# Row statistics, gain tiles and one step's order at the start of a hybrid decoder block

## The chip, the cores and the metric

The kernel runs on one core of one Trainium2 chip. The metric is the device time of one execution in microseconds (us). A core has five engines with their own instruction streams, each worked through in order: TensorE (PE; PEld is its weight load), VectorE (DVE), ScalarE (ACT), GpSimd (POOL) and SyncE (SP), which here only issues DMAs. SP, ACT and POOL issue DMAs, each into a queue of its own.

## The reference, cut to what matters

16 meta rows are put ahead of the 1024 rows of x (1040 rows of 1024 numbers). Each row is normalized and multiplied by a gain, and the result goes through one input projection and all that follows (a pooling mixer, forgetting attention with 8 heads, gates, an output projection, a residual and a final norm).

```python
def rmsnorm(x, g):
    xf = x.astype(jnp.float32)
    xf = xf * lax.rsqrt(jnp.mean(xf * xf, axis=-1, keepdims=True) + RMS_EPS)
    return (xf * g.astype(jnp.float32)).astype(x.dtype)

def hybrid_layer(x, norm_g, w_in, ...):
    h = rmsnorm(x, norm_g)
    proj = jnp.einsum('bld,dn->bln', h, w_in)
    u_pool, z_pool, q, k, v, z_attn, f_logit, g_pool, g_attn = jnp.split(proj, _split_points(), axis=-1)
    y_pool = causal_multiscale_pool(u_pool, pool_w, pool_scale) * jax.nn.silu(z_pool)
    ...
    y_attn = forgetting_attention(q, k, v, log_f).reshape(B, L, ATTN_WIDTH) * jax.nn.silu(z_attn)
    merged = (jax.nn.sigmoid(g_pool) * jnp.einsum('blc,cd->bld', y_pool, w_up_pool)
              + jax.nn.sigmoid(g_attn) * jnp.einsum('blc,cd->bld', y_attn, w_up_attn))
    return x + jnp.einsum('bld,de->ble', merged, w_out)
```

The kernel multiplies in pieces: every float32 operand is split into a high part and a low part, and a product is the sum of high by high, high by low and low by high.

## The kernel before, in words

The 1040 rows are cut into nine row tiles: tile 0 holds the 16 meta rows and 112 rows of x, tiles 1 to 7 hold 128 rows each, and tile 8 holds the last 16 rows. A row tile `xt` goes through these steps:

- `norm_load(i)` issues its load from SP's queue. Tile 0 has two loads: x (L184) and the meta rows (L185).
- `norm_stat` squares the row on ScalarE and sums it (L192, an activation and a read-out of the sum), adds epsilon on VectorE (L125) and takes the power -1/2 on GpSimd (L126). The tile `junk` takes the squares, which nobody reads.
- `norm_scale` multiplies, on VectorE, each half of the row by the statistic and by the gain (L197). The gain stands in PSUM as `gb`, spread over all 128 partitions by a matmul of ones with the row of gains (L399).
- `norm_t` transposes the tile on TensorE in two halves of four 128x128 blocks (L218; for the 16 rows of tile 8 L205, eight small ones), copies each half from PSUM as its high part `hh` on ScalarE (L220, L209) and takes the low part `hl` on VectorE (L221, L210). The halves use the two PSUM buffers `pt` of the pool psT in turn, and every third one the buffer `pn` of the pool psG: of tile 6 both halves go to `pt`, of tile 7 the first to `pn` and the second to `pt`. A buffer is free again when hh and hl of its former contents have been taken.

At the start ScalarE issues the load of the gains (L388) and does a tiny Square (L389), which brings its table load. The loads of row tiles 0 and 1 follow. TensorE does four dummy matmuls, the two for the gains, and one more (L395, L399). SP goes on with the raw weights of query, key and value of the first head pair (L404) between tiles 2 and 3. The weights are split into `whi` on ScalarE (L409) and `wlo` on GpSimd (L414).

Then a loop over twelve steps n = 0 to 11 projects query, key and value in turn for four stretches of rows (matmuls at L163, three groups of eight for each step: hh by whi, hl by whi, hh by wlo). The results are taken out of PSUM at L249 and L253 (query: `qa` on ScalarE, `ql` on VectorE), L271 and L274 (key: `ka` on both), and L278 (value: `vt` on ScalarE). After steps 4, 7 and 10, two blocks of the value are transposed (L287) and split into `V` (L292 on ScalarE, L293 on VectorE). In between, the loop handles the later row tiles:

```python
        i = {0: 2, 1: 3, 3: 4, 4: 5, 6: 6, 7: 7}.get(n)
        if i is not None:
            norm_t(i, xts[i], ntok(i))
        ...
        i = {1: 4, 2: 5, 4: 6, 5: 7, 6: 8}.get(n)
        if i is not None:
            norm_scale(xts[i], ntok(i), norm_stat(xts[i], ntok(i)))
```

So tile 7 is scaled at the end of step 5, tile 6 transposed in step 6, tile 8 scaled at the end of step 6, tile 7 transposed in step 7. The transposes of tile 8 stand inside step 8, after its first eight matmuls. Step 9 is the first that reads the rows of tiles 6 to 8.

All of this stands in a `manual_schedule` of all engines: each engine executes these instructions in the order of the program text. Behind it, only TensorE's order is written by hand (a planner inserts projection work between the steps of attention, by fixed costs); the other engines' instructions there are ordered by the framework's scheduler.

Of the kernel before, what the change touches and what calls it, by code (L numbers as in the profile page):

```python
# [8 lines left out]
F32 = mybir.dt.float32  # L9
F32R = mybir.dt.float32r  # L10
AF = mybir.ActivationFunctionType
ALU = mybir.AluOpType
AX = mybir.AxisListType

D = 1024
NM = 16
# [4 lines left out]
EPS = 1e-6  # L21
# [24 lines left out]
def r32(ap):  # L46
    return ap.bitcast(F32)
# [7 lines left out]
def tile_hybrid_block(ctx, tc, x, meta, norm_g, w_in, b_forget, pool_w, pool_scale,  # L55
                      w_up_pool, w_up_attn, w_out, final_g, out):
    nc = tc.nc
# [20 lines left out]
    sm = ctx.enter_context(tc.tile_pool(name="sm", bufs=2))  # L78
# [8 lines left out]
    psG = G_.enter_context(tc.tile_pool(name="psG", bufs=1, space=PS))  # L87
# [4 lines left out]
    epsp = cst.tile([128, 1], F32, name="epsp")  # L92
# [29 lines left out]
    def rstd_of(ss):  # L122
        n = ss.shape[0]
        r = sm.tile([128, 1], F32, name="rstd", bufs=4)
        nc.vector.tensor_scalar(r[:n], ss, EPS, None, op0=ALU.add)  # L125
        nc.gpsimd.tensor_tensor(r[:n], r[:n], epsp[:n], op=ALU.pow)  # L126
        return r
# [44 lines left out]
    def run(g):  # L172
        for _ in g:
            pass

    gb = psG.tile([128, 2, 512], F32, name="gb")
    junk = gp.tile([128, D], F32, name="junk", tag="g")

    def norm_load(i):
        c0 = i * 128  # L180
        n = min(128, L - c0)
        xt = ap_.tile([128, D], F32, name="xt", tag="s", bufs=6)
        if i == 0:
            nc.sync.dma_start(xt[NM:], x2[:128 - NM, :])  # L184
            nc.sync.dma_start(xt[:NM], meta)  # L185
        else:
            nc.sync.dma_start(xt[:n], x2[c0 - NM:c0 - NM + n, :])
        return xt

    def norm_stat(xt, n):  # L190
        ss = sm.tile([128, 1], F32, name="ss")
        nc.scalar.activation(junk[:n], xt[:n], AF.Square, scale=D ** -0.5, accum_out=ss[:n])  # L192
        return rstd_of(ss[:n])

    def norm_scale(xt, n, r):
        for j, (c0, c1) in enumerate(HALVES):
            nc.vector.scalar_tensor_tensor(xt[:n, c0:c1], xt[:n, c0:c1], r[:n], gb[:n, j],  # L197
                                           op0=ALU.mult, op1=ALU.mult)

    def norm_t(i0, xt, n):  # L200
        c0 = i0 * 128
        if n < 128:
            both = psT.tile([128, KO, n], F32, name="pt")
            for i in range(KO):
                nc.tensor.transpose(both[:, i, :], xt[:n, i * 128:(i + 1) * 128], ident[:n, :n])  # L205
            for j in range(2):
                h_ = hh4[j][:, :, c0:c0 + n]
                part = both[:, 4 * j:4 * j + 4]
                nc.scalar.activation(h_, part, AF.Copy)  # L209
                last = nc.vector.tensor_tensor(hl4[j][:, :, c0:c0 + n], part, r32(h_), op=ALU.subtract)  # L210
            return last
        for j in range(2):
            if (2 * i0 + j) % 3 == 2:
                pt = psG.tile([128, 4, 128], F32, name="pn")
            else:
                pt = psT.tile([128, 4, 128], F32, name="pt")
            for i in range(4):
                nc.tensor.transpose(pt[:, i, :n], xt[:n, (4 * j + i) * 128:(4 * j + i + 1) * 128], ident[:n, :n])  # L218
            h_ = hh4[j][:, :, c0:c0 + n]
            nc.scalar.activation(h_, pt[:, :, :n], AF.Copy)  # L220
            last = nc.vector.tensor_tensor(hl4[j][:, :, c0:c0 + n], pt[:, :, :n], r32(h_), op=ALU.subtract)  # L221
        return last
# [6 lines left out]
    def zero_q(p):  # L229
        for e in range(2):  # L230
            nc.gpsimd.memset(r32(QL[p, e])[rows(e)[1]], 0.0)
# [12 lines left out]
    def q_piece(p, w, t0, t1):  # L244
        c0, c1 = t0 - NM, t1 - NM
        ps = yield from g_proj(w, t0, t1)

        def hi(e, r):
            nc.scalar.activation(QA[p, e][r, c0:c1], ps[rows(e)[0]], AF.Copy, scale=0.125)  # L249

        def lo(e):
            a, _ = rows(e)
            nc.vector.scalar_tensor_tensor(QL[p, e][a, c0:c1], ps[a], 0.125, r32(QA[p, e][a, c0:c1]),  # L253
                                           op0=ALU.mult, op1=ALU.subtract)

        for group in EVAC[p > 0]:
            for e in group:
                hi(e, rows(e)[0])
                if not p:
                    hi(e, rows(e)[1])  # L260
            for e in group:
                lo(e)
                if p:
                    hi(e, rows(e)[1])

    def k_piece(p, w, t0, t1):
        ps = yield from g_proj(w, t0, t1)
        for group in EVAC[p > 0]:
            for e in group:
                a, o = rows(e)  # L270
                nc.scalar.activation(KA[p, e][a, t0:t1], ps[a], AF.Copy)  # L271
            for e in group:
                a, o = rows(e)
                nc.vector.tensor_tensor(KA[p, e][o, t0:t1], ps[a], r32(KA[p, e][a, t0:t1]), op=ALU.subtract)  # L274

    def v_piece(p, w, t0, t1):
        ps = yield from g_proj(w, t0, t1)
        nc.scalar.activation(VT[p][:, t0:t1], ps, AF.Copy)  # L278

    def v_alloc(p):  # L280
        for e in range(2):
            V[p, e] = ap_.tile([KB, NB, 2, 64], F32R, name="V", bufs=3)
# [102 lines left out]
    onesr = ap_.tile([128, 128], F32R, name="onesr", tag="m")  # L385
    nc.vector.memset(r32(onesr), 1.0)
    grow = ap_.tile([1, D], F32, name="grow", tag="t")
    nc.scalar.dma_start(grow, norm_g)  # L388
    nc.scalar.activation(junk[:1, :2], r32(onesr)[:1, :2], AF.Square)  # L389
    xts = {0: norm_load(0), 1: norm_load(1)}  # L390
    warm = psG.tile([128, 4, 128], F32, name="pn")

    def warm_up(n):
        for _ in range(n):
            nc.tensor.matmul(warm, onesr, onesr[:, None, :].to_broadcast([128, 4, 128]), start=True, stop=True)  # L395

    warm_up(WARM[0])
    for j, (c0, c1) in enumerate(HALVES):
        nc.tensor.matmul(gb[:, j], r32(onesr)[:1], grow[:, c0:c1], start=True, stop=True)  # L399
    warm_up(WARM[1])  # L400

    def load_raw(col, pool=None, tag="raw"):
# [4 lines left out]
    def split_hi(raw, pool, tag):  # L407
        hi = pool.tile([128, KO, 128], F32R, name="whi", tag=tag)
        nc.scalar.activation(hi, raw, AF.Copy)  # L409
        return hi  # L410

    def split_lo(raw, hi, pool, tag):
        lo = pool.tile([128, KO, 128], F32R, name="wlo", tag=tag)
        nc.gpsimd.tensor_tensor(lo, raw, r32(hi), op=ALU.subtract)  # L414
        return hi, lo

    rq = load_raw(COL_Q)
    xts[2] = norm_load(2)
    rk = load_raw(COL_K)
    xts[3] = norm_load(3)  # L420
    rv = load_raw(COL_V, gp, "g")

    def ntok(i):
        return min(128, L - 128 * i)

    alloc_k(0)
    for i in range(2):
        norm_scale(xts[i], 128, norm_stat(xts[i], 128))
    hq_ = split_hi(rq, wp, "wh")
    norm_t(0, xts[0], 128)  # L430
    wq = split_lo(rq, hq_, wp, "wl")
# [4 lines left out]
    for i in (2, 3):  # L436
        norm_scale(xts[i], 128, rs[i - 2])
# [4 lines left out]
    for n, (kind, t0, t1) in enumerate(todo):  # L442
        if n + 4 < 9:
            xts[n + 4] = norm_load(n + 4)
        if kind == "q":
            run(q_piece(0, wq, max(NM, t0), t1))
        elif kind == "k":
            run(k_piece(0, wk, t0, t1))
        else:
            g = v_piece(0, wv, t0, t1)  # L450
            if n == 8:
                for _ in range(KO):
                    next(g)
                norm_t(8, xts[8], ntok(8))
            run(g)
# [3 lines that stand above are left out]
        if n == 0:  # L459
            hv_ = split_hi(rv, gp, "g")  # L460
            wv = split_lo(rv, hv_, gp, "g")
            VT[0] = gp.tile([128, L], F32, name="vt", tag="g")
            v_alloc(0)
        i = {1: 4, 2: 5, 4: 6, 5: 7, 6: 8}.get(n)
        if i is not None:
            norm_scale(xts[i], ntok(i), norm_stat(xts[i], ntok(i)))
        if n == 2:
            zero_q(0)
        if n == 4:
            wf = at_.tile([128, KO, H], F32, name="wf", bufs=1)  # L470
            nc.sync.dma_start(wf, w_in2[:, :, COL_F:COL_F + H])
        if n == 8:
            wfs = at_.tile([128, KO, 2 * H], F32R, name="wfs", bufs=1)
            nc.vector.tensor_copy(wfs[:, :, :H], wf)
            nc.vector.tensor_tensor(wfs[:, :, H:], wf, r32(wfs[:, :, :H]), op=ALU.subtract)
        if n in (4, 7, 10):
            run(v_blocks(0, 2 * (n // 3) - 2, 2 * (n // 3)))
# [507 lines left out]
    for n, s in enumerate(steps):  # L985
# [10 lines left out]
        j, a = s  # L996
# [148 lines left out]
```

## Time and profile before

| what | value |
|---|---|
| time, 3 runs | 737.64, 738.9 and 739.29 us, median 738.9 |
| the profiled execution: time | 738.82 us |
| the profiled execution: span, first to last instruction | 737.1 us |
| granted TensorE clock, mean | 0.999 |
| TensorE busy | 725.2 us, 98% of the span |
| VectorE, ScalarE, GpSimd busy | 531.6, 375.8, 305.9 us |
| input stage (to the last projection of the first head pair) | 0 to 56.5 us |

A row of the timeline has the start in us, the duration of the group in us, the engine (a "q" behind it is its queue, where DMAs are issued), the line, the operation, the tile written and the tiles read, shapes, and the number of instructions. A bracket at its end is the idle time of the engine ahead of it, and what ended that. A row of the busy time by stage has the stretch, its length, and for TensorE, its weight load, VectorE, ScalarE and GpSimd the busy time with the count, then the granted clock, the share of time in which the DMA engines were busy, and GB/s. A row of the DMA issues has the KB of each and the time from issue to landing in us. A row of the groups has the line, the shapes, the count, the busy time in us and the mean in ns of one instruction, then the idle time ahead.

### The profile page before, as it was taken

What the parts mean: (1) busy time and instruction counts of PE and PEld (TensorE: products, weight loads), DVE (VectorE), ACT (ScalarE), POOL (GpSimd) and SP (SyncE); (2) the same over time, 40 slices, a digit from 0 to 9 for tenths busy, and PEclk for the clock granted to TensorE, in tenths of its full rate; (3) what the DMA queues carried; (4) which work ended last, traced back from release to release, by engine and by line L of the source; (5) the groups of instructions that cost most, each with busy time, mean ns of one, the idle gap of its engine ahead of it and who ended that gap; (6) DMA issues with size and microseconds to landing.
All of it is one profiled execution on the core that took longest, in us unless ns stands there. A gap on an engine that the chain in (4) does not pass through costs nothing.

```text
span 737.1 us, 10620 instructions
## 1 busy us (share of the span) xinstructions
PE 725.2 (98%) x3686; PEld 624.2 (85%) x3686; DVE 531.6 (72%) x991; ACT 375.8 (51%) x736; POOL 305.9 (42%) x362
## 2 busy tenths in 40 slices
PE   8999999999999999999999999999999999999996
PEld 6997999988889898889888888888887888888885
DVE  4753578859769878788798688687288554887775
ACT  6652555356456645556554564462545422626445
POOL 4322145465435547336436374283349011006243
PEclk9999999999999999999999999999999999999999
DMA  9201123321452355411542346227485357672006
GB/s 302 61 6 53 28 77 88 98 80 30 109 158 51 94 106 107 120 50 42 177 99 84 98 135 152 73 79 240 138 234 187 113 189 269 222 262 72 1 1 229
DMA packets 82312, 86.89 MB, mean 118 GB/s; under 512 B 9889, under 2 KB 61089, under 8 KB 82226
## 3 DMA queue, kind: packets, MB, share of 16 engines
q1 hardware_dynamic: 78272, 77.29, 34.0%
q0 software_dynamic: 2112, 4.19, 3.6%
q10 hardware_dynamic: 1874, 4.72, 1.7%
q8 instruction: 29, 0.48, 0.3%
q14 instruction: 25, 0.20, 0.1%
HBM read 67.12 MB, written 27.46 MB: 128 GB/s over the span
## 4 chain that ended last, share of the span: by engine, by line
PE 88%; DVE 3%; ACT 1%; issue 1%; POOL 1%; POOLq 0%; ACTq 0%; DVEq 0%
PE pj L163 66%; PE pj L1025 8%; PE po L669 5%; PE ps L609 3%; PE ps L608 2%; PE pt L1025 2%; PE pj L494 1%; POOL yl L136 1%; PE pj L287 0%; DVE S L648 0%; ACT whi L149 0%; DVE pl L653 0%; DVE pt L639 0%; DVE S L615 0%; DVE mt L629 0%
## 5 line engine op out<-in xcount | busy, mean ns | idle before, releaser
L151 POOL TENSOR_TENSOR wlo<-raw,whi 128x256 fp32r<-128x256 f32 x148 | 123.5, 879 | 187.2 <-ACT whi L149 95.9
L163 PE MATMUL pj<-hh,whi 128*128 128x512 f32 (+5 forms) x768 | 178.9, 361 | 0.7 <-DVE V L293 0.4
L163 PE MATMUL pj<-hl,whi 128*128 128x512 f32 (+5 forms) x768 | 175.8, 358 | 0.0
L163 PE MATMUL pj<-hh,wlo 128*128 128x512 f32 (+5 forms) x768 | 173.7, 356 | 0.0
L163 PEld LDWEIGHTS pj<-hh,whi 128*128 128x128 f32 x768 | 132.4, 190 | 17.5 <-PE pj L287 0.6
L163 PEld LDWEIGHTS pj<-hh,wlo 128*128 128x128 f32 x768 | 132.2, 188 | 17.1
L163 PEld LDWEIGHTS pj<-hl,whi 128*128 128x128 f32 x768 | 132.2, 189 | 16.6
L653 DVE TENSOR_TENSOR pl<-S,ph 128x512 fp32r<-128x512 f32 (+4 forms) x112 | 88.3, 806 | 14.0 <-ACT ph L652 13.5
L661 POOL TENSOR_TENSOR acc<-acc,S 128x272 f32<-128x272 f32 (+4 forms) x80 | 77.1, 963 | 8.9 <-ACT S L649 3.7
L617 ACT ACTIVATE S<-ps,negc 128x400 f32<-128x400 f32 (+2 forms) x96 | 49.1, 514 | 48.1 <-DVE S L615 40.5
L649 ACT ACTIVATE S<-S 128x512 f32<-128x512 f32 (+4 forms) x112 | 49.7, 478 | 33.6 <-DVE S L648 33.4
L624 DVE TENSOR_TENSOR m<-m,S 128x272 f32<-128x272 f32 (+4 forms) x80 | 40.9, 512 | 23.1 <-ACT S L617 21.3
L652 ACT ACTIVATE ph<-S 128x512 fp32r<-128x512 f32 (+4 forms) x112 | 51.7, 479 | 9.4 <-PE po L669 8.6
L149 ACT ACTIVATE whi<-raw 128x1024 fp32r<-128x1024 f32 x37 | 39.1, 1056 | 33.6 <-PE pj L163 26.0
L648 DVE TENSOR_TENSOR S<-S,pt 128x512 f32<-128x512 f32 (+4 forms) x112 | 51.7, 498 | 0.8
L873 DVE TENSOR_TENSOR rl<-pj,rl 128x512 f32<-128x512 f32 x32 | 22.1, 690 | 31.5 <-PE pj L163 31.5
L669 PE MATMUL po<-pl,V 128*128 128x512 f32 (+4 forms) x112 | 37.5, 335 | 0.1
L609 PE MATMUL ps<-ql,ka 128*128 128x512 f32 (+4 forms) x112 | 37.4, 334 | 0.0
L615 DVE SCALAR_TENSOR_TENSOR S<-ps,negc,mask 128x128 f32<-128x128 f32 (+2 forms) x72 | 23.7, 330 | 18.8 <-PE ps L609 17.9
L608 PE MATMUL ps<-qa,ka 128*128 128x512 f32 (+4 forms) x112 | 35.9, 321 | 1.2 <-ACT S L617 1.2
L325 ACT ACTIVATE st<-pj 128x512 f32<-128x512 f32 x40 | 23.7, 593 | 26.1 <-PE pj L163 18.8
L1025 PE MATMUL pj<-opy 128*128 128x512 f32 (+1 forms) x168 | 36.2, 374 | 0.0
(187 smaller groups left out, 1101.2 us busy)
## 6 DMA issues: line engine op xcount, KB each, us to landing
raw<-in_w_in_dram SPq DMA_DIRECT2D x40, 512.0 KB, 4.0
sp_gp<-st SPq DMA_DIRECT2D x16, 256.0 KB, 2.0
td<-in_w_out_dram POOLq DMA_DIRECT2D x4, 1024.0 KB, 10.2
sp_ga<-st SPq DMA_DIRECT2D x16, 256.0 KB, 2.0
rl<-sp_gp SPq DMA_DIRECT2D x8, 512.0 KB, 5.3
rl<-sp_ga SPq DMA_DIRECT2D x8, 512.0 KB, 4.7
W<-td SPq DMA_DIRECT2D x8, 512.0 KB, 5.3
xr<-in_x_dram SPq DMA_DIRECT2D x8, 512.0 KB, 4.2
```

The source lines that it names most:

```text
L151: ins = nc.gpsimd.tensor_tensor(lo[:, k:k + 2], raw[:, k:k + 2], r32(hi[:, k:k + 2]), op=ALU.subtract)
L163: nc.tensor.matmul(ps, a, b, start=(i == 0), stop=(i == len(seq) - 1))
L608: nc.tensor.matmul(ps[:kb, c0:], ka[:, k0:k0 + kb], qa[:, q0 + c0:q0 + 512], start=True, stop=False)
L609: nc.tensor.matmul(ps[:kb, c0:], ka[:, k0:k0 + kb], ql[:, q0 + c0:q0 + 512], start=False, stop=True)
L617: nc.scalar.activation(s[:kb, f0:], ps[:kb, f0:], AF.Identity, bias=nb_)
L648: nc.vector.tensor_tensor(s[:kb, c0:], s[:kb, c0:], self.pm[:kb, c0:], op=ALU.subtract)
L649: exps.append(nc.scalar.activation(s[:kb, c0:], s[:kb, c0:], AF.Exp))
L652: nc.scalar.activation(ph[:kb, c0:], s[:kb, c0:], AF.Copy)
L653: dves.append(nc.vector.tensor_tensor(pl[:kb, c0:], s[:kb, c0:], r32(ph[:kb, c0:]), op=ALU.subtract))
L661: accs.append(nc.gpsimd.tensor_tensor(acc[:kb, c0:], acc[:kb, c0:], s[:kb, c0:], op=ALU.add))
L669: nc.tensor.matmul(self.po[:, c0:], v, r[:kb, c0:], start=(b == 0 and i == 0), stop=(b == self.nb - 1 and i == 1))
L1025: nc.tensor.matmul(ps, pick(A_, k, p)[:, i * 128:(i + 1) * 128], pick(B_, k, q)[:, c0:c1], start=start and n == 0, stop=n == 11, skip_grou ...
```

## The change

Four edits, all in the input stage. The gain tile `gb` becomes two tiles, one for each half of the row. The meta rows are loaded by ScalarE's queue; in ScalarE's program this load stands behind the tiny Square of L389. Row tile 0 gets its statistic from `norm_stat2`: ScalarE squares and sums the first half of the row, VectorE the second, and one VectorE instruction adds both sums and epsilon. And tile 8 (16 rows) is squared and scaled at the end of step 5, behind tile 7, and no longer at the end of step 6.

```diff
-    gb = psG.tile([128, 2, 512], F32, name="gb")
+    gb = [psG.tile([128, 512], F32, name=f"gb{j}") for j in range(2)]
...
             nc.sync.dma_start(xt[NM:], x2[:128 - NM, :])
-            nc.sync.dma_start(xt[:NM], meta)
+            nc.scalar.dma_start(xt[:NM], meta)
...
+    def norm_stat2(xt, n):
+        ss = [sm.tile([128, 1], F32, name="ss") for _ in range(2)]
+        nc.scalar.activation(junk[:n, :512], xt[:n, :512], AF.Square, scale=D ** -0.5, accum_out=ss[0][:n])
+        nc.vector.scalar_tensor_tensor(junk[:n, 512:], xt[:n, 512:], 1.0 / D, xt[:n, 512:], op0=ALU.mult, op1=ALU.mult,
+                                       accum_out=ss[1][:n])
+        r = sm.tile([128, 1], F32, name="rstd", bufs=4)
+        nc.vector.tensor_scalar(r[:n], ss[0][:n], ss[1][:n], EPS, op0=ALU.add, op1=ALU.add)
+        nc.gpsimd.tensor_tensor(r[:n], r[:n], epsp[:n], op=ALU.pow)
+        return r
+
     def norm_scale(xt, n, r):
         for j, (c0, c1) in enumerate(HALVES):
-            nc.vector.scalar_tensor_tensor(xt[:n, c0:c1], xt[:n, c0:c1], r[:n], gb[:n, j],
+            nc.vector.scalar_tensor_tensor(xt[:n, c0:c1], xt[:n, c0:c1], r[:n], gb[j][:n],
...
-        nc.tensor.matmul(gb[:, j], r32(onesr)[:1], grow[:, c0:c1], start=True, stop=True)
+        nc.tensor.matmul(gb[j], r32(onesr)[:1], grow[:, c0:c1], start=True, stop=True)
...
     for i in range(2):
-        norm_scale(xts[i], 128, norm_stat(xts[i], 128))
+        norm_scale(xts[i], 128, (norm_stat if i else norm_stat2)(xts[i], 128))
...
-        i = {1: 4, 2: 5, 4: 6, 5: 7, 6: 8}.get(n)
-        if i is not None:
+        for i in {1: (4,), 2: (5,), 4: (6,), 5: (7, 8)}.get(n, ()):
             norm_scale(xts[i], ntok(i), norm_stat(xts[i], ntok(i)))
```

## The prediction

> **What bounds the kernel now.** I read the page first. It says that one engine, TensorE, fills the span, so an edit counts only by what it does to the idle time of TensorE.
>
> ```profile
> span 737.1 us, 10620 instructions
> PE 725.2 (98%) x3686; PEld 624.2 (85%) x3686; DVE 531.6 (72%) x991; ACT 375.8 (51%) x736; POOL 305.9 (42%) x362
> PE 88%; DVE 3%; ACT 1%; issue 1%; POOL 1%; POOLq 0%; ACTq 0%; DVEq 0%
> ```
>
> Next the busy time by stage, over the projections of the first head pair:
>
> ```profile
> 12.50:41.40 28.90, 28.88 (x240) 28.39 (x238) 20.27 (x41) 22.18 (x48) 10.84 (x13) 1.00 0.38 118
> ```
>
> From 12.5 to 41.4 us TensorE is busy for 28.88 of 28.90 us. All four edits lie before 48 us, so they can act in two places only: on when this stretch starts (the front), and on what happens behind 41.4 us, where TensorE first waits again. The timeline gives both. The front:
>
> ```profile
> 0.80 0.53 ACTq L388 DMA_DIRECT2D grow<-in_norm_g_dram  x1
> 1.25 0.41 SPq L185 DMA_DIRECT2D xt<-in_meta_tokens_dram  x1
> 2.17 0.43 SPq L404 DMA_DIRECT2D raw<-in_w_in_dram  x1
> 2.65 0.20 ACT L389 ACTIVATE junk<-onesr 1x2 f32<-1x2 f32 x1
> 4.95 1.06 ACT L192 ACTIVATE junk<-xt 128x1024 f32<-128x1024 f32 x1 [2.09 <-DMA xt<-in_meta_tokens_dram]
> 7.20 1.41 DVE L197 SCALAR_TENSOR_TENSOR xt<-xt,rstd,gb 128x512 f32<-128x512 f32 x2 [0.92 <-PE gb L399]
> 7.63 1.06 ACT L192 ACTIVATE junk<-xt 128x1024 f32<-128x1024 f32 x1 [1.53 <-DMA xt<-in_x_dram]
> 9.30 1.06 ACT L409 ACTIVATE whi<-raw 128x1024 fp32r<-128x1024 f32 x1 [0.53 <-DMA raw<-in_w_in_dram]
> 10.26 1.07 ACT L220 ACTIVATE hh<-pt 128x512 fp32r<-128x512 f32 x2
> 11.70 0.71 PEld L218 LDWEIGHTS pt<-ident,xt 128*128 128x128 f32 x4 [0.53 <-DVE hl L221]
> ```
>
> Read it backwards. The last transposes ahead of the first projection (11.70) wait for the low half hl of row tile 0, that one for hh (10.26), and hh stands on ScalarE behind whi (9.30), which waits for raw, the query weights. So the front hangs on the landing of the query weights at 9.3 us and not on row tile 0, whose normalization three of the edits speed up: its scaling is done by 8.61 and the transposes follow it.
>
> The end of the stretch, VectorE from 38 to 47 us:
>
> ```profile
> 38.76 1.41 DVE L197 SCALAR_TENSOR_TENSOR xt<-xt,rstd,gb 128x512 f32<-128x512 f32 x2 [0.66 <-POOL rstd L126]
> 40.08 0.85 DVE L253 SCALAR_TENSOR_TENSOR ql<-pj,qa 64x256 fp32r<-64x256 f32 x2
> 40.97 1.29 DVE L221 TENSOR_TENSOR hl<-pt,hh 128x512 fp32r<-128x512 f32 x2
> 42.17 0.13 DVE L125 TENSOR_SCALAR rstd<-ss 16x1 f32<-16x1 f32 x1
> 42.95 1.39 DVE L197 SCALAR_TENSOR_TENSOR xt<-xt,rstd,gb 16x512 f32<-16x512 f32 x2 [0.65 <-POOL rstd L126]
> 44.38 0.86 DVE L274 TENSOR_TENSOR ka<-pj,ka 64x256 fp32r<-64x256 f32 x2
> 46.47 0.28 DVE L293 TENSOR_TENSOR V<-pj,V 128x128 fp32r<-128x128 f32 x1
> ```
>
> TensorE beside it:
>
> ```profile
> 40.90 0.60 PE L218 MATMUL pn<-ident,xt 128*128 128x128 f32 x4
> 41.71 0.66 PE L218 MATMUL pt<-ident,xt 128*128 128x128 f32 x4 [0.22 <-DVE hl L221]
> 42.34 1.19 PE L163 MATMUL pj<-hh,whi 128*128 128x256 f32 x8
> 43.79 0.39 PE L205 MATMUL pt<-ident,xt 16*128 16x16 f32 x4 [0.26 <-issue]
> 44.40 0.42 PE L205 MATMUL pt<-ident,xt 16*128 16x16 f32 x4 [0.23 <-DVE xt L197]
> 44.75 1.22 PE L163 MATMUL pj<-hl,whi 128*128 128x256 f32 x8
> 45.81 1.07 PE L163 MATMUL pj<-hh,wlo 128*128 128x256 f32 x8
> 47.23 1.36 PE L163 MATMUL pj<-hh,whi 128*128 128x272 f32 x8 [0.35 <-ACT hh L209]
> ```
>
> And ScalarE:
>
> ```profile
> 40.34 1.04 ACT L192 ACTIVATE junk<-xt 16x1024 f32<-16x1024 f32 x1
> 46.79 0.28 ACT L292 ACTIVATE V<-pj 128x128 fp32r<-128x128 f32 x1 [3.38 <-DVE V L293]
> 46.96 0.22 ACT L209 ACTIVATE hh<-pt 128x64 fp32r<-128x64 f32 x1
> ```
>
> The reader is to see that VectorE is the slow one here. It works through one row in program order from 38.76 to 46.75 us, its only gap of size the 0.65 us of waiting for GpSimd's power. TensorE waits for it four times: 0.22 us for the low half of row tile 6 (which frees the PSUM buffer for the second half of tile 7), 0.26 and 0.23 us around the transposes of the 16 rows, and 0.35 us at 47.23, by way of ScalarE's hh.
>
> **The change, part by part.** Durations are of the profiled execution: span 737.1 us, its own time 738.82 us, against a median of 738.9 us (737.64 to 739.29). The two differ by 0.08 us, so sums made against 738.82 stand for the median as well. About 0.2%, 1.48 us, is what a measurement of this kernel can tell from no change.
>
> *Two PSUM tiles for the gains.* The first scaling at 7.20 waits for both gain matmuls, since they write one tile; afterwards its first half waits for the first matmul only. No instruction is added. The cover is the query weights: hh stands behind whi until 10.26 us, whatever the transposes of tile 0 do. Taken at nothing. Without the cover it could give at most the 0.92 us of idle time ahead of 7.20.
>
> *Half of the first square on VectorE.* ScalarE's 1.06 us become about half; VectorE gets one 128x512 multiply. The nearest row for that:
>
> ```profile
> L1060 DVE SCALAR_TENSOR_TENSOR o<-xr,sst,fgb 128x512 f32<-128x512 f32 x8 | 6.0, 748 | 2.9 <-POOL sst L1058 2.9
> ```
>
> VectorE is idle before 6 us, so 0.75 us run beside ScalarE's half and the statistics come some 0.3 us sooner (0.75 against 1.06). The same cover: nothing. No row has a sum kept by VectorE; even at double, 1.5 us, the half would end only 0.44 us after the whole square did, still under the cover.
>
> *Meta rows on ScalarE's queue.* This moves one DMA issue past two others. The two issue slots of SP from 1.25 to 2.17 take 0.92 us, so one is 0.46 us, and row tile 1 and the query weights (2.17) are issued that much sooner. ScalarE gets an issue behind the table load and the tiny Square at 2.65, so at about 2.7 us instead of 1.25; queued behind it is the first square, which waits for these rows. How soon they land:
>
> ```profile
> xt<-in_meta_tokens_dram SPq DMA_DIRECT2D x1, 64.0 KB, 3.6
> out_dram<-o ACTq DMA_DIRECT2D x8, 256.0 KB, 2.8
> rl<-sp_zp ACTq DMA_DIRECT2D x4, 512.0 KB, 6.6
> ```
>
> Before: 1.25 + 3.6, the square at 4.95. Afterwards between 2.7 + 2.8 = 5.5 and 2.7 + 6.6 = 9.3 us; I take 5.5 to 6.3 (3.6 for the same 64 KB, less because these rows no longer stand behind tile 0 in one queue). With the halved square the scaling starts near 7.2 again. The cover holds while the half square is over when tile 1's starts at 7.63, that is for a landing up to about 6.7 us.
>
> What can be gained is an earlier landing of the query weights. ScalarE idles 0.53 us ahead of 9.30, and the issue comes 0.46 us sooner, so 0.46 is the upper end. But the engines that carry the bytes are full soon:
>
> ```profile
> 2.00:2.50 0.50, 0.50 (x3) 0.40 (x2) 0.00 (x0) 0.50 (x1) 0.00 (x0) 1.00 0.69 213
> 2.50:3.00 0.50, 0.50 (x3) 0.18 (x1) 0.00 (x0) 0.35 (x2) 0.00 (x0) 1.00 1.01 393
> ```
>
> From 2.5 us their share is 1.01; before, 0.31 of half a microsecond, 0.15 us, is free, and the meta bytes still have to pass. I take a gain of 0.1 us at the front; ends 0 and 0.46. [...]
>
> *The 16 rows scaled one step sooner.* Moved are: the square (1.04 us) on ScalarE, the addition (0.13), GpSimd's power, and two scalings (1.39) on VectorE. Their load is not moved, and nothing else of SP's or GpSimd's queue is passed. In program order they now follow the scaling of tile 7, ahead of ql and hl of step 6. On ScalarE the square passes qa and hh of tile 6, which come 1.0 us later; ka, behind them, keeps its place. On VectorE the moved block runs from 42.17 to 44.38, 2.21 us with its wait for GpSimd, a wait that now has ql and hl queued behind it. So ql goes from 40.08 to 42.29, hl of tile 6 from 40.97 to 43.18, and its first half ends 2.21 us later. TensorE waits for exactly that half at 41.71: the transposes of tile 7's second half move to 43.92. TensorE stands from 41.50 (end of the row at 40.90) to 43.92, 2.4 us in place of 0.2.
>
> What comes back: the 16 rows are long scaled when their transposes are reached. From 42.34, eight matmuls at the pace of 44.75 to 45.81 (1.06 us) and eight small transposes at twice the 0.35 us from 44.40 to 44.75 end at 44.10, not 44.75: 0.65 us. At 47.23 the 0.35 us of idle time go as well, since VectorE's V (46.47) and with it hh (46.96) keep their times: the same work, only reordered, lies ahead of them. Together 1.0 us. At the mean pace of the stretch from 12.50 to 41.40 (28.88 us for 240, 0.96 us for eight) the two are 0.75 and 47.23 - 45.81 - 0.96 = 0.46, together 1.2 us. Net 2.21 less 1.0 to 1.2 = +1.0 to +1.2 us; I take +1.0, since the mean of many is the surer pace. The lower bound is 0: hh at 46.96 cannot come sooner by a reordering. The upper is 2.2, nothing recovered.
>
> Sum: -0.1 + 0 + 0 + 1.0 = +0.9 us; 738.82 + 0.9 = 739.7 us. Behind 47 us TensorE is full again, and I see nothing that would take the time up.
>
> **The rivals.**
> *A swap that costs nothing:* the wait that comes is as long as those that go, because ql and hl find VectorE sooner than I reckon (a shorter power, say), and the front gives 0 to 0.1. 738.8 us. For it: the work on VectorE is the same. Against it: TensorE does 4 us of work between tile 7's transposes and step 9, and that cannot start before hl.
> *Slower, the long stand costs TensorE's rate:* two rows of the same eight transposes differ by a factor of 1.9:
>
> ```profile
> 8.01 1.97 PE L218 MATMUL pt<-ident,xt 128*128 128x128 f32 x8 [0.17 <-DVE xt L197]
> 37.28 1.03 PE L218 MATMUL pt<-ident,xt 128*128 128x128 f32 x8
> ```
>
> Early, after idle time, TensorE is slow. If 2.4 us of standing bring that back for two groups of eight matmuls, 2 x 1.06 x 0.9 = 1.9 us are added: 741.6 us. It decides from about half a group of eight on, 0.6 us above my sum. Against it: none of the waits shown behind 41 us, up to 0.35 us, slowed what followed by more than a tenth, though they are short. [...]
> *Slower, the meta rows late:* a landing at 8.3 us, toward the 6.6 us row, puts the half square at 8.3 to 9.0, tile 1's square with its read-out at 9.0 to 10.2, and whi at 10.3 and not 9.3: +1.0 us at the front, so 740.8 us. It decides from a landing at 7.9 us on. For it: the engines are full by then (1.01). Against it: that row is of 512 KB, this load of 64 KB.
> *Faster, the stalls go and none comes:* if the transposes did not wait for hl of tile 6, 1.0 to 1.2 us are won, with the whole 0.46 at the front -1.5 to -1.7, 737.2 us; it decides from 0.3 us at the front on. For it: this is where TensorE waited. Against it is the row at 41.71.
>
> **How the numbers follow.** My case 0.60, of which 0.08 lie beyond +1.48 us; the free swap 0.14; the rate 0.10; the late rows 0.10; the faster one 0.06. Slower: 0.08 + 0.10 + 0.10 = 0.28; faster 0.06; the same 0.52 + 0.14 = 0.66. My case's own range is +0.5 (1.0 less the whole 0.46) to +2.1 us (nothing recovered, 2.2 less 0.1): 739.3 to 740.9. The range given, 738.1 to 741.3, takes in the free swap and the late rows, with the spread of single runs, and leaves out the faster case and most of the rate case.
>
> **What would show it.** Right: one wait of TensorE at L218 for hl, over 2 us, between the two halves of tile 7; no wait at L205 or for hh of the 16 rows; whi of the query weights starting within 0.2 us of 9.2; step 9 starting near 48.1 us. Wrong: that wait under 1 us, whi later than 9.6, the groups of eight behind the stand at well over 1.06 us, or a new wait after 48 us.

## The result, and the profile after

The changed kernel is slower: median 742.84 us of six runs (739.63, 742.66, 742.72, 742.95, 743.07, 743.23) against 738.47 us of six runs of the kernel before; ratio 1.0053, 95% interval 1.0041 to 1.0065. Forecast were 739.7 us, within 738.1 to 741.3. One of the six came out at 739.63 us, and that one alone had a mean granted TensorE clock of 0.999; the other five had 0.993 to 0.996. The profiled execution took 742.66 us with a span of 740.9 us, 3.8 us more than before. (On two of the chips used below a few executions of the kernel before lay 1.6 to 3.5 us above its median; medians and intervals are given for that reason.)

The page after has TensorE as full as before, so the shares don't tell where 3.8 us went:

```profile
span 740.9 us, 10622 instructions
PE 726.6 (98%) x3686; PEld 626.3 (85%) x3686; DVE 529.6 (71%) x993; ACT 376.3 (51%) x736; POOL 307.9 (42%) x362
```

The front, from the timeline of the changed kernel (L197 is ScalarE's half of the first square, L207 the scaling that was L197, L230 and L231 take hh and hl, L228 transposes):

```profile
1.44 0.34 ACTq L185 DMA_DIRECT2D xt<-in_meta_tokens_dram  x1
6.86 0.63 ACT L197 ACTIVATE junk<-xt 128x512 f32<-128x512 f32 x1 [3.99 <-DMA xt<-in_meta_tokens_dram]
7.93 1.06 ACT L192 ACTIVATE junk<-xt 128x1024 f32<-128x1024 f32 x1 [0.34 <-DVE rstd L201]
8.57 1.41 DVE L207 SCALAR_TENSOR_TENSOR xt<-xt,rstd,gb 128x512 f32<-128x512 f32 x2 [0.67 <-POOL rstd L202]
8.99 1.04 ACT L419 ACTIVATE whi<-raw 128x1024 fp32r<-128x1024 f32 x1
10.52 0.60 ACT L230 ACTIVATE hh<-pt 128x512 fp32r<-128x512 f32 x1 [0.50 <-PE pt L228]
12.78 0.71 PEld L228 LDWEIGHTS pt<-ident,xt 128*128 128x128 f32 x4 [0.53 <-DVE hl L231]
13.54 2.25 PE L163 MATMUL pj<-hh,whi 128*128 128x240 f32 x8
15.59 1.91 PE L163 MATMUL pj<-hl,whi 128*128 128x240 f32 x8
17.30 1.42 PE L163 MATMUL pj<-hh,wlo 128*128 128x240 f32 x8
18.55 0.60 PE L228 MATMUL pt<-ident,xt 128*128 128x128 f32 x4
```

The meta rows, issued at 1.44, arrive at 6.86 us, where the whole of tile 0 had been there at 4.95. The scaling slips from 7.20 to 8.57. The query weights, by contrast, no longer hold whi up: it follows tile 1's square at 8.99 without a wait. And hh of tile 0, which stood behind whi before, now waits for the transposes (10.52). The first projection starts 1.07 us later than at 12.47. The same three groups of matmuls before:

```profile
12.47 2.24 PE L163 MATMUL pj<-hh,whi 128*128 128x240 f32 x8
14.51 1.46 PE L163 MATMUL pj<-hl,whi 128*128 128x240 f32 x8
15.80 1.07 PE L163 MATMUL pj<-hh,wlo 128*128 128x240 f32 x8
16.71 0.60 PE L218 MATMUL pt<-ident,xt 128*128 128x128 f32 x4
```

After, the second and the third are slower too (1.91 and 1.42 for 1.46 and 1.07): TensorE comes to full rate later, and by the transposes of tile 2 the delay is 18.55 - 16.71 = 1.84 us. This second part is not the edit's alone. In another execution with the same front (the change with its stand filled, below) the second and the third group, at 14.19 and 15.09 us, took 1.06 us each. And in three kernels below whose meta rows stand in SP's queue as before, the second group took 1.48 us at 14.59 (the step alone), 1.07 us at 14.42 (the change, meta rows back) and 1.64 us at 14.99 (stand part filled). So 1.07 us can be laid to the front in this profile, and the other 0.8 us hang on when the full rate comes, which differs from execution to execution. The delay stays until tile 7 (42.67 for 40.90, 1.77 us):

```profile
42.65 1.39 DVE L207 SCALAR_TENSOR_TENSOR xt<-xt,rstd,gb 16x512 f32<-16x512 f32 x2 [0.65 <-POOL rstd L126]
43.98 0.85 DVE L263 SCALAR_TENSOR_TENSOR ql<-pj,qa 64x256 fp32r<-64x256 f32 x2
44.85 1.29 DVE L231 TENSOR_TENSOR hl<-pt,hh 128x512 fp32r<-128x512 f32 x2
42.67 0.60 PE L228 MATMUL pn<-ident,xt 128*128 128x128 f32 x4
45.60 1.12 PE L228 MATMUL pt<-ident,xt 128*128 128x128 f32 x4 [2.33 <-DVE hl L231]
46.80 2.06 PE L163 MATMUL pj<-hh,whi 128*128 128x256 f32 x8
48.78 0.67 PE L215 MATMUL pt<-ident,xt 16*128 16x16 f32 x8
49.38 1.22 PE L163 MATMUL pj<-hl,whi 128*128 128x256 f32 x8
51.34 1.15 PE L163 MATMUL pj<-hh,whi 128*128 128x272 f32 x8
```

Here is the stand that was forecast: 2.33 us of waiting for hl of tile 6, which VectorE takes behind the scaling of the 16 rows and ql. But the group behind it takes 2.06 us where it took 1.19, and step 9 starts 4.11 us later than before, at 51.34 (0.27 us of that come back later, as the time is 3.84 us longer). The busy time by stage of the same kernel tells why (the column behind GpSimd's is the granted clock):

```profile
43.30:45.33 2.03, 0.00 (x0) 0.00 (x0) 1.99 (x5) 1.36 (x4) 0.00 (x0) 1.00 0.00 0
45.33:48.74 3.41, 3.14 (x14) 2.96 (x14) 3.14 (x7) 0.92 (x3) 0.00 (x0) 0.50 0.00 0
48.74:52.00 3.26, 3.26 (x31) 3.19 (x31) 1.07 (x5) 0.96 (x4) 0.00 (x0) 1.00 0.00 0
```

For 3.41 us, from 45.33 to 48.74, the granted clock is 0.50. So the rival of the lost rate came true. The meta rows were late, too, but not by the path of the rival that has them late: whi started sooner than before (8.99 for 9.30) and not at 10.3 us.

### The profile page after: what moved, and what is told of

It is laid out like the page before. It is cut to its first block, busy times and chain, and to the rows that moved or that the text cites. A ratio compares the mean times of both kernels' runs of the same rounds, so it can differ in the third digit from the quotient of the medians.

```text
span 740.9 us, 10622 instructions
## 1 busy us (share of the span) xinstructions
PE 726.6 (98%) x3686; PEld 626.3 (85%) x3686; DVE 529.6 (71%) x993; ACT 376.3 (51%) x736; POOL 307.9 (42%) x362
## 4 chain that ended last, share of the span: by engine, by line
PE 92%; DVE 3%; issue 2%; ACT 1%; POOL 1%; POOLq 0%; ACTq 0%; DVEq 0%
PE pj L163 70%; PE pj L1034 8%; PE po L678 5%; PE ps L618 3%; PE ps L617 2%; PE pt L1034 2%; PE pj L503 1%; PE pt L228 1%; POOL yl L136 1%; PE pj L297 0%; DVE S L657 0%; ACT whi L149 0%; DVE pl L662 0%; PE pn L228 0%; DVE xt L207 0%
```

## The experiments

Each ran five rounds beside the kernel before on the same chip. "Low clock" counts the executions with a mean granted clock of 0.996 or less (of the kernel before, two of its 101 executions beside the experiments, both on the chip of the first four, at 742.1 and 742.2 us). The last two columns are of the profiled execution: the start of tile 7's first transposes (40.90 us before), and the time from there to the first matmul of step 9 (6.33 us before), which shows the step. The first of the two is no measure of the front: in the five kernels of this table whose meta rows stand in SP's queue as before, the profiled executions give 40.63 to 41.77 us, since the front differs from execution to execution (whi of the query weights at 9.22 us with the meta rows back and at 9.39 in the step alone, the first projection at 12.38, 12.55 and, with the stand part filled, 12.95).

| kernel | median us | before on that chip | ratio, 95% interval | low clock | tile 7 at | to step 9 |
|---|---|---|---|---|---|---|
| the change | 742.84 | 738.47 | 1.0053 (1.0041 to 1.0065) | 5 of 6 | 42.67 | 8.67 |
| step alone | 740.57 | 738.74 | 1.0022 (1.0006 to 1.0037) | 7 of 12 | 40.89 | 7.27 |
| front alone | 739.39 | 738.74 | 1.0005 (0.9995 to 1.0015) | 0 of 11 | 41.58 | 6.34 |
| meta queue alone | 739.34 | 738.74 | 1.0006 (0.9997 to 1.0015) | 0 of 11 | 41.64 | 6.34 |
| change, meta rows back | 739.65 | 738.74 | 1.0017 (1.0007 to 1.0027) | 4 of 12 | 40.73 | 9.41 |
| step alone, stand filled | 738.97 | 738.65 | 1.0005 (0.9996 to 1.0014) | 0 of 11 | 41.77 | 7.26 |
| step alone, stand part filled | 740.85 | 738.96 | 1.0021 (1.0007 to 1.0035) | 2 of 12 | 41.38 | 7.28 |
| change, stand filled | 739.72 | 738.95 | 1.0013 (1.0004 to 1.0021) | 0 of 11 | 41.05 | 7.26 |
| meta rows first | 740.07 | 738.65 | 1.0018 (1.0009 to 1.0027) | 0 of 11 | 42.27 | 6.34 |
| statistic sooner | 738.33 | 738.65 | 0.9996 (0.9987 to 1.0004) | 0 of 11 | 40.63 | 6.03 |
| meta first, gains on GpSimd | 741.16 | 738.95 | 1.0032 (1.0020 to 1.0045) | 0 of 6 | 44.02 | 6.04 |
| meta first, gains first on SP | 737.99 | 738.96 | 0.9983 (0.9974 to 0.9993) | 0 of 11 | 40.17 | 6.04 |

**The step alone.** The kernel before with only this:

```diff
-        i = {1: 4, 2: 5, 4: 6, 5: 7, 6: 8}.get(n)
-        if i is not None:
+        for i in {1: (4,), 2: (5,), 4: (6,), 5: (7, 8)}.get(n, ()):
```

> Only the 16 rows scaled one step sooner; the front is that of before. My theory (the stand behind tile 7's first half costs 2.2 us less about 1.2 us that comes back, and in most executions TensorE's clock falls to half for one stretch of 3.4 us, 1.7 us more): front unchanged, a wait of TensorE for hl of 2.2 us near 41.6 us, and two groups of times, about 739.4 us where the clock holds and about 741.1 us where it falls. Rival A, the stand costs its length alone and the lost clock belongs to something else: one group at 739.4 us. Rival B, the step costs nothing and all of the loss is the front's: 738.5 us.

Measured: twelve runs in three groups that the mean clock parts. Five with 0.998 to 0.999: median 739.13 us. Four with 0.996: 740.9 us. Three with 0.993 to 0.994: 742.3 us (one of them 744.75). The profiled execution is of the first group:

```profile
40.89 0.60 PE L218 MATMUL pn<-ident,xt 128*128 128x128 f32 x4
43.82 0.66 PE L218 MATMUL pt<-ident,xt 128*128 128x128 f32 x4 [2.33 <-DVE hl L221]
44.45 1.20 PE L163 MATMUL pj<-hh,whi 128*128 128x256 f32 x8
45.58 0.67 PE L205 MATMUL pt<-ident,xt 16*128 16x16 f32 x8
48.16 1.15 PE L163 MATMUL pj<-hh,whi 128*128 128x272 f32 x8
```

The same stand of 2.33 us, no low clock, the group behind it at 1.20 us, and step 9 at 48.16 us, where the prediction put 48.1. So the stand by itself costs 0.9 us here (0.7 by the end of that group, which took 1.36 us before and takes 1.15); the rest of this kernel's loss goes with the low clock. Rivals A and B fall.

**The front alone**: the changed kernel with the step undone (the diff above, reversed). **The meta queue alone**: the kernel before with `nc.scalar.dma_start(xt[:NM], meta)`.

> The three edits of the front (gain tiles, meta rows on ScalarE's queue, half of the first square on VectorE); the 16 rows scaled where they were. My theory: the meta rows land near 6.8 us, the first projection starts about 1.1 us later than before and TensorE gets warm later, so that the third group of matmuls ends 1.1 to 1.8 us later; no wait for hl of over 0.3 us, no stretch at half clock after it; 739.6 to 740.3 us. Rival B (all of the loss is the front's): 742 us or more.

> Only the meta rows moved to ScalarE's queue; the whole first square on ScalarE. My theory (the queue makes the front late): the rows land near 6.8 us and not 4.9, the first square starts there and is whole, so whi of the query weights comes at 9.2 to 9.5 us and the first projection 1 to 1.6 us later than before: 739.6 to 740.3 us. Rival C, it is the halved square that makes the front late (tile 1's square waits until VectorE has read the two sums, 0.34 us, and VectorE's order is changed): the front starts within 0.2 us of before, 738.5 us.

Measured: 0.65 us and 0.60 us above before, not resolved from no change, and less than I expected. The timeline of the meta queue alone:

```profile
6.38 1.06 ACT L192 ACTIVATE junk<-xt 128x1024 f32<-128x1024 f32 x1 [3.52 <-DMA xt<-in_meta_tokens_dram]
8.62 1.04 ACT L409 ACTIVATE whi<-raw 128x1024 fp32r<-128x1024 f32 x1
9.19 1.97 PE L218 MATMUL pt<-ident,xt 128*128 128x128 f32 x8 [1.36 <-DVE xt L197]
10.34 0.60 ACT L220 ACTIVATE hh<-pt 128x512 fp32r<-128x512 f32 x1 [0.68 <-PE pt L218]
13.31 0.70 PE L163 MATMUL pj<-hh,whi 128*128 128x240 f32 x4
```

With a whole square and one gain tile the same picture: the rows arrive at 6.4 us, whi is 0.7 us sooner than at 9.30, and hh waits for transposes. The same path stands in all four traces with the meta rows behind the tiny Square (landing at 6.0 to 6.9 us), so the queue is what changes the front, and rival C falls; the halved square and the gain tiles change nothing that these runs can tell.

**The change, meta rows back**: the changed kernel with `nc.sync.dma_start(xt[:NM], meta)`.

> The changed kernel with the meta rows back on SP's queue: gain tiles, halved first square and the sooner step. My theory (queue): the rows land near 4.9 us, the front starts within 0.2 us of before, and what is left is the stand, as in the kernel with the step alone: 739.4 us where the clock holds, 741.1 us where it falls. Rival C (the halved square makes the front late): first projection 1 us later, 740.5 to 742.5 us.

Measured: 739.65 us, with eight executions of unimpaired clock at a median of 739.3 us, two with 0.996 (740.3 and 741.3 us) and two with 0.994 (741.8 and 742.3 us). The front is that of before (hh at 10.19 us stands behind whi again). The profiled execution fell into the last group; its busy time by stage:

```profile
45.20:51.90 6.70, 6.70 (x35) 6.44 (x34) 2.38 (x8) 1.00 (x4) 0.00 (x0) 0.50 0.00 0
```

Half clock over at least 6.70 us, about twice the 3.41 us of the first case. By its mean clock that is the third group of the step alone: a loss of 1.5 to 1.8 us at a mean clock of 0.996, which the first case had, and 2.7 to 3.2 us at 0.993 to 0.994. Why the clock is down for 3.41 us in one execution and for 6.70 or more in another, no run tells.

**The step alone, stand filled.** Ten dummy matmuls take the place of the idle time:

```diff
         for j in range(2):
+            if j and fill is not None:
+                for _ in range(10):
+                    nc.tensor.matmul(fill, onesr, onesr[:, None, :].to_broadcast([128, 4, 128]), start=True, stop=True)
             if (2 * i0 + j) % 3 == 2:
```

`fill` is given for tile 7 only: the PSUM tile of the value transposes that follow, taken one call sooner.

> The kernel with the sooner step alone, and ten dummy matmuls of 128x512 on TensorE between the two halves of tile 7's transposes, into the PSUM buffer that the next value transposes overwrite: about 2.2 us of work in the place of the stand. My theory (idle time of TensorE in the stand makes the clock fall): the step's own cost of 0.5 us stays, the clock holds in every execution, one group of times at 739.1 to 739.5 us with mean clocks of 0.997 to 0.999, and none near 740.9 or 742.3 us. Rival D (the clock falls for another reason, such as the phase of the executions or what VectorE does there): the same three groups as with the step alone, 739.1, 740.9 and 742.3 us.

```profile
41.77 0.60 PE L221 MATMUL pn<-ident,xt 128*128 128x128 f32 x4
42.12 2.52 PE L215 MATMUL pj<-onesr 128*128 128x512 f32 x10
44.69 0.66 PE L221 MATMUL pt<-ident,xt 128*128 128x128 f32 x4
```

Measured: one group, 738.38 to 739.91 us, all clocks 0.997 or above. The transposes are just as late (7.26 us to step 9 and not 6.33), but with work of no use in the gap the clock stays: it is the idleness, and rival D falls. (Filled and unfilled kernels ran on different chips, so the counts alone would not exclude the chip; but where the clock fell in a trace, it fell around the end of the stand: at 45.33 us with the next matmuls at 45.60, and by 45.20 with the next at 43.66.) The step's own cost is then 0.3 us by the medians, with an interval from -0.3 to 1.0, and 0.7 to 0.9 by the traces.

**The step alone, stand part filled**: the same with four dummies, which leaves a wait of 1.41 us.

> The kernel with the sooner step alone, and four dummy matmuls in place of ten, so that TensorE stands for about 1.4 us and not 2.3. [...]

Measured: two of twelve executions with a low clock (0.995 and 0.996), but they don't show that a wait of 1.41 us is enough for it. They took 742.9 and 743.4 us, and four others took 741.5 to 741.8 us at clocks of 0.997 and more, as five of before on this chip took 740.6 to 741.1. The profiled execution is one of the four, and its trace has another long wait, far behind the input stage; before and then here:

```profile
567.91 1.20 PE L163 MATMUL pj<-yl,whu 128*128 128x512 f32 x4 [0.58 <-POOL yl L136]
570.83 1.20 PE L163 MATMUL pj<-yl,whu 128*128 128x512 f32 x4 [2.31 <-POOL yl L136]
```

A second stand of 2.31 us, then, over 500 us behind the edits. In this execution the clock held through it (0.998 in the mean). That it, and not the 1.41 us in the input stage, brought the clock down in the two low ones fits their times (a further 1.2 and 1.7 us above the four) and the two low ones of before on another chip, but neither was profiled. The six shorter executions (739.4 to 740.2 us) all have clocks of 0.997 and more. So whether a stand of 1.41 us can bring the clock down stays open.

**The change, stand filled**: the changed kernel with the ten dummies.

> The changed kernel whole, with the ten dummy matmuls in the stand. My theory (the loss is 0.65 us of front, 0.3 to 0.7 us of step, and 1.8 or 3.4 us of half clock in most executions): with the clock held the first two are left, one group of times 0.9 to 1.4 us above before, 739.5 to 740.0 us, mean clocks of 0.997 to 0.999. Rival G (front and step together cost more than each alone): 741 us or more with the clock held.

Measured: one group, 739.29 to 740.44 us, 0.77 us above before. With the clock held the whole change costs about what front and step cost alone (0.65 and 0.32 by their medians; the interval of the 0.77 goes from 0.3 to 1.6), so nothing of size is hidden in it, and rival G falls.

**Meta rows first.** To see whether ScalarE's queue is slow or the issue too late:

```diff
+    xt0 = ap_.tile([128, D], F32, name="xt", tag="s", bufs=6)
+    nc.scalar.dma_start(xt0[:NM], meta)
     nc.scalar.dma_start(grow, norm_g)
```

> The kernel before, with the meta rows issued by ScalarE as its first instruction at 0.8 us, ahead of the gains, and so ahead of row tile 1 on SP. My theory (the rows were late because they were issued behind row tile 1 and its 512 KB, and the engines serve what was issued first): they land by 4.6 us, the query weights are issued 0.46 us sooner and land 0.3 to 0.5 us sooner, and the front starts 0 to 0.4 us sooner than before, 738.3 to 738.7 us. Rival E (a load on ScalarE's queue is served late beside a full SP queue, whenever it is issued): they land at 6 us or later and the time is that of the queue edit alone, 739.3 us.

The DMA issues of that kernel, and then its timeline:

```profile
xt<-in_meta_tokens_dram ACTq DMA_DIRECT2D x1, 64.0 KB, 3.4
```

```profile
5.00 3.78 PE L400 MATMUL gb<-grow,onesr 1*128 1x512 f32 x4 [1.61 <-DMA grow<-in_norm_g_dram]
8.12 1.06 ACT L410 ACTIVATE whi<-raw 128x1024 fp32r<-128x1024 f32 x1 [0.53 <-DMA raw<-in_w_in_dram]
8.87 1.41 DVE L196 SCALAR_TENSOR_TENSOR xt<-xt,rstd,gb 128x512 f32<-128x512 f32 x2 [2.41 <-PE gb L400]
```

The landing came as in my theory: issued at 0.80 us the rows land after 3.4 us, on the same queue, and the query weights are in at 8.1 us, 1.2 us sooner than before. Rival E falls for the meta rows. The time missed: 740.07 us, as now the gains, issued second, land at 5.0 us, their matmuls end at 8.8 us, and the scaling waits for them. I had not counted what the moved load was put ahead of.

**The statistic sooner.** The square, addition and power of the 16 rows at the end of step 5, their scaling left where it was:

```diff
-            norm_scale(xts[i], ntok(i), norm_stat(xts[i], ntok(i)))
+            norm_scale(xts[i], ntok(i), r8 if i == 8 else norm_stat(xts[i], ntok(i)))
+        if n == 5:
+            r8 = norm_stat(xts[8], ntok(8))
```

> The kernel before, with the statistic of the 16 rows (square, addition, power) at the end of step 5 and their scaling left at the end of step 6. My theory (VectorE's order sets the end of this stretch, and a wait for GpSimd's power in it is dead time): 0.65 us of waiting leave VectorE's chain, the low half of tile 6 comes 0.2 to 0.4 us later, no stand of over 0.6 us, the waits at the transposes of the 16 rows fall, the clock holds, and the first matmul of step 9 starts 0.2 to 0.7 us sooner: 738.1 to 738.5 us. Rival F (any move of this row's work ahead of step 6 delays the low half of tile 6 as much as it saves): 738.7 us or more.

```profile
40.30 0.86 DVE L253 SCALAR_TENSOR_TENSOR ql<-pj,qa 64x256 fp32r<-64x256 f32 x2 [0.35 <-ACT qa L249]
42.39 1.38 DVE L197 SCALAR_TENSOR_TENSOR xt<-xt,rstd,gb 16x512 f32<-16x512 f32 x2
41.93 0.66 PE L218 MATMUL pt<-ident,xt 128*128 128x128 f32 x4 [0.71 <-DVE hl L221]
43.69 0.66 PE L205 MATMUL pt<-ident,xt 16*128 16x16 f32 x8
46.66 1.36 PE L163 MATMUL pj<-hh,whi 128*128 128x272 f32 x8 [0.25 <-ACT hh L209]
```

Measured: the wait for GpSimd is out of VectorE's chain, tile 7 waits 0.71 us, the 16 rows not at all, and the way to step 9 is 0.30 us shorter: in the sense of my theory. The time, 0.3 us lower, is not resolved.

**Two versions of both.** The statistic sooner and the meta rows first, with the gains issued by GpSimd, and then as SP's first DMA:

```diff
-    nc.scalar.dma_start(grow, norm_g)
+    nc.scalar.dma_start(xt0[:NM], meta)
+    nc.gpsimd.dma_start(grow, norm_g)      # second version: nc.sync
```

> A version that should beat both kernels: the statistic of the 16 rows one step sooner and their scaling where it was, the meta rows as ScalarE's first DMA, and the gains on GpSimd's queue so that they don't stand behind the meta rows. My theory: meta rows by 4.5 us, query weights by 8.2 us and not 9.3, the gain matmuls not later than before, the first projection 0.5 to 0.9 us sooner than before and step 9 0.8 to 1.3 us sooner: 737.3 to 737.9 us. Rival E (what is issued second lands late, on any queue): the gains land at 5 us, the first scaling waits for their matmuls to near 9 us as when they stood behind the meta rows, and the front is 1.3 us later: 739.7 us.

> The statistic of the 16 rows one step sooner, the meta rows as ScalarE's first DMA, and the gains as SP's first, ahead of row tile 0. My theory (what is issued first lands first): gains by 3.4 us, row tile 0 half a microsecond later than before at near 5 us, the query weights 0.3 to 0.8 us sooner than before, first projection 0 to 0.6 us sooner, and step 9 another 0.5 us from the sooner statistic: 737.6 to 738.3 us. Rival I (row tile 0, now later, takes the place of the query weights as what the front waits for): no gain over the sooner statistic alone, 738.3 to 738.7 us.

Measured: with GpSimd 741.16 us, slower, against my theory and as rival E has it: its issue comes at 1.35 us and the gains land 5.3 us later, so the first scaling starts at 10.61. With SP 737.99 us, ratio 0.9983 (0.9974 to 0.9993): faster than both kernels, as forecast, by 1.0 us (0.8 if the five long executions of before on this chip are left out). Its timeline:

```profile
4.92 1.06 ACT L191 ACTIVATE junk<-xt 128x1024 f32<-128x1024 f32 x1 [2.20 <-DMA xt<-in_x_dram]
8.35 1.06 ACT L410 ACTIVATE whi<-raw 128x1024 fp32r<-128x1024 f32 x1 [0.67 <-DMA raw<-in_w_in_dram]
11.98 1.51 PE L163 MATMUL pj<-hh,whi 128*128 128x240 f32 x8
```

Row tile 0 is there at 4.92 us as before, the query weights 0.95 us sooner, and the first projection starts 0.5 us sooner than in the profile of before. In three other kernels with the meta rows on SP's queue it starts at 12.38, 12.55 and 12.95 us, so the size of this gain is known only roughly.

## Why the prediction was wrong

*Where the time went.* At step 9 the profiled execution is 4.11 us late, of which 3.84 are left at the end. 1.77 us came at the front (1.07 to the first projection, the rest because the full rate came later in this execution). From tile 7 to step 9 it took 8.67 us and not 6.33, 2.34 us more; the step alone with a full clock took 7.27, 0.94 more, so 1.4 are the half clock. By medians: 0.65 for the front alone, 0.3 to 0.4 for the step with the clock held, and 1.5 to 1.8 us more at a mean clock of 0.996, 2.7 to 3.2 at 0.993 to 0.994. Five of the six fell, four of them to 0.993 and 0.994: 0.65 + 0.35 + 3.2 = 4.2 of the 4.37 us between the medians.

*Gain tiles, half of the first square: right.* With the meta rows back the first transposes started at 7.63 us and not 8.01, yet hh stood behind whi until 10.19, and the first projection started at 12.38 us against 12.47; the cover was there and they gave nothing that could be told.

*Meta rows on ScalarE's queue: wrong.* The failed step is the cover. I let it end where a landing after 6.7 us would delay tile 1's square, with the query weights landing at 9.2 us. But the same edit takes tile 0's delay and the weights' gain in opposite directions: with the queue edit alone whi started 0.7 us sooner (0.3 in the changed kernel, there behind tile 1's square), and the transposes, pushed back by 0.5 to 1.4 us in the four traces, became the last. A cover that the edit itself moves has to be placed anew before a delay is put under it. Wrong as well was the issue: 1.44 us, during the table load, and not 2.7 behind it; yet the rows landed at 6.0 to 6.9 us in the four traces, three of them later than the 5.5 to 6.3 I took. The later experiment fits with their standing behind row tile 1 (issued at 1.25). The term was -0.1 us; it measured +0.6 to +0.65 in the two kernels that had it without the step, neither resolved from nothing.

*The 16 rows one step sooner: right in place, and by the trace nearly in size.* The stand was to be 2.4 us behind tile 7's first half and was 2.33; step 9 was to start at 48.1 us and did at 48.16 with the front of before. The term of +1.0 us measured 0.7 to 0.9 in that trace and 0.3 to 0.4 by medians. (Of the four waits laid to VectorE, the 0.26 us at 43.79 has "issue" behind it in its row; it went all the same.)

*The rate: the failed step with the most weight.* My sum has nothing for it. I priced it as a rival (1.9 us; measured 1.4 to 1.8 with 3.41 us at half clock, and 2.7 to 3.2 with 6.70 or more, which I had not thought of) but gave it 0.10, on the ground that no wait shown slowed what followed. Those waits were up to 0.35 us, so the rows said nothing on one of 2.3. In the changed kernel 2.03 us without a matmul (43.30 to 45.33) stood ahead of the 3.41 us at a clock of 0.50. With this case at the 7 in 12 that the step alone shows, I would have forecast slower and not the same.

## What to carry to other kernels

A reordering that makes a full TensorE stand for 2 us can cost more than 2 us less what comes back: here it halved the clock, for 3.41 us in one trace and 6.70 us or more in another, in some executions and not in others, and then the spread of the runs, read beside their mean clocks, shows it before any timeline does. One profile is one execution: where a landing or the first full rate moves from execution to execution (with one and the same front the first square started at 6.86 us in one and at 6.03 in another, and the second group took 1.91 and 1.06 us), a difference of the front is read from medians. When a load is moved to another queue, look at what is then issued ahead of it on all queues and behind it on the new one, and place every cover again with the times that the edit itself changes.

## What the runs showed of the hardware

The idleness that brought the clock down was short: 2.03 us right ahead of the low stretch in the changed kernel (43.30 to 45.33, then 0.50 until 48.74). Kernels with a stand of 2.33 us in their profile had a low mean clock in 16 of 30 executions, and with dummy matmuls in the gap in 0 of 22.

Why only some executions fall is not shown. With the same stand of 2.33 us in all three traces, the granted clock was 0.50 for 3.41 us in the changed kernel, 0.50 for at least 6.70 us with the meta rows back, and 1.00 in the step alone from 43.80 to 47.20 us, where the group behind the stand took 1.20 us. The wait of 2.31 us at 570 us in the part filled kernel left the pace behind it at 1.20 us for four matmuls, as before. So the length of the stand alone does not tell these executions apart.

64 KB on ScalarE's queue took 2.1 to 3.4 us when issued at 0.80 us (three traces) and 4.8 to 5.3 us when issued at 1.4 us, behind 512 KB of another queue (three traces; in the fourth the square behind it started at 6.03 us). And taking 64 KB out of SP's queue let whi of the query weights start at 8.1 to 8.4 us in the three kernels with the meta rows first, against 9.22 to 9.39 us in three traces with the meta rows on SP's queue (before, the step alone, the meta rows back): 1.1 us by the means, more than the 0.46 us of the issue slot, which I had held for the upper end. In one of the three the gains took that slot and the weights were issued only 0.13 us sooner, yet they came 0.95 us sooner. Why these runs gave more than the issue time is open.
